# Residual rows and softmax sums turned by VectorE and DMA instead of TensorE in a two-layer hybrid trunk

## The chip, the core and the metric

The kernel runs on one core of a Trainium2 chip. The core has TensorE (PE, a 128x128 matmul array with its own weight loads, PEld), VectorE (DVE), ScalarE (ACT), GpSimd (POOL) and SyncE (SP), which here issues every DMA. SBUF and PSUM have 128 partitions; matmul results land in PSUM, in banks of 128 x 512 floats. The metric is the device time of one execution in microseconds (us), as the median of several runs.

## The reference

One sequence of 1024 tokens with 1024 features passes two layers. Layer 0 mixes by gated linear attention, layer 1 by sparse attention with an indexer that keeps the 256 best keys of every query; each is followed by a residual, a layer norm and a gated input of per-layer embeddings.

```python
for i in range(DEPTH):                       # DEPTH = 2
    y = gla_mixer(x, ...) if i == 0 else dsa_mixer(x, ...)
    x = layer_norm(ALPHA * x + y, ln_g[i], ln_b[i])      # ALPHA = 4 ** 0.25
    x = x + (p[i] @ ple_w[i]) * jax.nn.sigmoid(x @ ple_gate_w[i])
```

In the sparse attention, 16 heads of 128 share one key and one value head. For every head

```python
probs = jax.nn.softmax(logits, axis=-1)      # over the kept keys
o = probs @ v_sel
...
return (o * jax.nn.silu(z)) @ w_out          # over all 16 heads
```

All is float32 in and out.

## The kernel before, in words

**Numbers.** A float32 matmul is done as three matmuls of a faster 32-bit format: every operand is split into a high part (a ScalarE copy) and a low part (a VectorE subtraction), and hi*hi, hi*lo and lo*hi are added in PSUM. A *block* is one product of a 1024-row weight with 512 tokens: 8 x 3 = 24 matmuls of 512 columns (`fm_block`, L441).

**Order.** Tokens go in two halves of 512. Layer 0 runs half 0 and half 1, each as four heads (`v_phase`, `qk_phase`, `core_steps`, `out_phase`) and a `tail` (L905: layer norm applied, turned to features by rows, gate). After each tail come the indexer's and the shared key and value projections (`small_head` L1003, `small_kv` L1050). Then layer 1 runs half 0 and half 1, each as 17 slots and a tail. In a slot the head's attention steps lie between the projection blocks of other heads.

**The order is written by hand.** `Flow` (L48 on) keeps a clock `fl.now` that advances with the TensorE work issued so far, 512/2400 us for a matmul of 512 columns. Steps are put in a heap with a due time (`fl.at`, `after`, `chain`), and are issued between matmuls when `fl.now` has passed it and what they require is there (`fl.req`, `fl.ripe`); `fl.need` issues what is due later until a condition holds. Engines execute in the order of issue, so a step that waits holds what is behind it on its engine or queue. Weight tiles are loaded and split ahead of use by `Weights.pace`, at most two or three tiles ahead, through SP's queue. In layer 1 the weights come split already, from DRAM.

**The residual of layer 1.** The tail of layer 0 writes x2 (the input of layer 1) to DRAM by features, `x2s[k]` with k = 0..7, 128 features x 1024 tokens. Layer 1 adds its projections by tokens, to a tile `y` of 128 tokens x 4 x 1024. `residual` (L1489) loads two `x2s[k]` in each of the slots 0 to 3, turns each by four TensorE transposes into a PSUM bank (L1500) and copies them into `y` on ScalarE, times ALPHA (L1501). `accumulate` (L805) adds the projection on VectorE (L827), and `norm_steps` (L854) takes statistics (L869), powers on POOL (L863 to L866) and applies them in place, for two of the four token blocks on ScalarE (L877), for two on VectorE (L879). `xpose` in the tail (L916) turns the normalised `y` back by TensorE.

**The softmax sums.** A head's exponentials leave a sum per query in a 128x4 tile `sm`. `inverse` (L1602) takes reciprocals, `turn` transposes 128x4 to 4x128 on TensorE, ScalarE copies it out of PSUM (L1616), SP stores it to a DRAM `row` (L1617), and `to_all` (L1621) loads it back to all 128 partitions (L1625); the gate `z` is multiplied by it (L1647). `inverse` is due 3.0 before the end of the slot that computes the head's logits, `to_all` 3.5 (half 0) or 5.0 (half 1) into the next. A slot lasts 3.6 (half 0) or 8.6 (half 1) plus 5.12 for each block in it: two blocks in slots 0 to 3, three in slots 4 to 14.

**The pattern already used for squares.** In layer 0, `core_steps` turns an output of 128x512 as 32x32 squares on VectorE (L731), stores it by four DMAs, one for each 32 partitions (L750), and loads it back in one DMA (L756). The stores and the load put the squares in their places, and the reading instructions (L769 to L775) go by runs of 32.

**Start.** `start_half` (L1225) loads X by rows and the first two weight tiles, and the feeder splits X; with `feed_by(feeder, 0.0, 0.0)` (L1288) one row is issued at every step.

**Loads for layer 1's half 1.** `feed_x2` (L1481) loads `x2s[k]` one by one into a pair of buffers and splits them, beginning 21 us into the last projections of half 0.

## Time and profile before

| | us |
|---|---|
| median of 3 runs (1944.57 to 1944.95) | 1944.63 |
| the profiled execution | 1945.97 |
| its span, first to last instruction | 1944.2 |
| TensorE busy | 1924.8 |
| VectorE busy | 1481.8 |
| ScalarE busy | 1014.5 |
| POOL busy | 55.2 |

DMA moved 480.50 MB, 247 GB/s on average, all through SP's queue. The profile lists groups of instructions by line, engine and operation, with tile names: `out<-in`, shapes, count, busy time, mean length in ns, and the idle time of the engine ahead of them with what ended it. TensorE's instructions all stand on L58 (matmul) or L62 (transpose), so they are told apart by their tiles. Matmuls overlap: one of 512 columns lasts some 390 ns, and the next starts before it ends, so cost is read from start to start. In a timeline each row gives the start, the length, the engine, the line, the operation and, in brackets, the engine's idle time ahead of it with its releaser. SPq is SP's queue of DMA issues; a row's length there is the time to issue, not to move data.

### The profile page before, as it was taken

Reading aid. Unit: us, or ns where it says so; the run is one execution under the profiler, and the core shown is the slowest. Engines: PE = TensorE matmul, PEld = TensorE weight load, DVE = VectorE, ACT = ScalarE, POOL = GpSimd, SP = SyncE. Lnnn points to the kernel's source line nnn. Section 1 sums busy time; section 2 is a strip of 40 time slices with the busy share of each in tenths; the row PEclk is TensorE's granted clock in tenths of the full one; section 3 lists DMA queues with packets and bytes.
Section 4 is the critical chain, followed back from the end, with each engine's and each line's share of the span. In section 5 each row is a group of like instructions: output and inputs, shape, how many; then the busy total and the mean of one; then the engine's idle time right before and its main releaser. Section 6 shows DMA issues by size and latency. Waiting matters only on the chain.

```text
span 1944.2 us, 26708 instructions
## 1 busy us (share of the span) xinstructions
PE 1924.8 (99%) x8912; PEld 1596.4 (82%) x8912; DVE 1481.8 (76%) x3039; ACT 1014.5 (52%) x1930; POOL 55.2 (3%) x115
## 2 busy tenths in 40 slices
PE   9999999999999999999999999999999999999999
PEld 7888888888788888888888888888878888888877
DVE  5777666696778888888859987778797887777873
ACT  5564636445564646464635676766443554434432
POOL 0000000010000000000100000000000000000000
PEclk9999999999999999999999999999999999999999
DMA  4567776767668777677686588877867998888873
GB/s 155 201 222 229 221 226 214 227 210 268 227 196 266 226 212 233 220 226 218 207 304 222 194 308 292 276 271 259 317 221 236 365 323 300 299 297 300 294 260 144
DMA packets 195818, 480.50 MB, mean 247 GB/s; under 512 B 22496, under 2 KB 39008, under 8 KB 189536
## 3 DMA queue, kind: packets, MB, share of 16 engines
q1 hardware_dynamic: 195680, 478.79, 73.8%
q8 instruction: 70, 1.15, 0.2%
q14 instruction: 68, 0.56, 0.1%
HBM read 338.98 MB, written 139.72 MB: 246 GB/s over the span
## 4 chain that ended last, share of the span: by engine, by line
PE 88%; DVE 4%; ACT 4%; DMA 2%; issue 1%; SPq 0%; POOL 0%; ACTq 0%; DVEq 0%
PE pb L58 66%; PE o L58 8%; PE U L58 6%; PE S L58 6%; DMA wlo<-wls 1%; PE tr L58 1%; ACT x L926 1%; DVE wlo L191 0%; DVE bn L869 0%; DMA xst<-x2s 0%; DMA y<-in_x_T 0%; DVE y L827 0%; PE pb L62 0%; PE ix L58 0%; DMA row<-uf 0%
## 5 line engine op out<-in xcount | busy, mean ns | idle before, releaser
L58 PE MATMUL pb<-x,whi 128*128 128x512 f32 x2272 | 705.4, 391 | 1.1 <-DVE x L411 1.0
L58 PEld LDWEIGHTS pb<-x,whi 128*128 128x128 f32 x2272 | 418.2, 188 | 81.2 <-DVE x L411 2.2
L58 PE MATMUL pb<-x,wlo 128*128 128x512 f32 x1136 | 442.8, 390 | 0.0
L58 PE MATMUL pb<-whi,u 128*128 128x512 f32 x1024 | 339.9, 392 | 1.5 <-ACT u L419 0.8
L58 PEld LDWEIGHTS pb<-x,wlo 128*128 128x128 f32 x1136 | 213.2, 188 | 45.7 <-DVE wlo L191 0.4
L58 PEld LDWEIGHTS pb<-whi,u 128*128 128x128 f32 x1024 | 192.1, 188 | 41.4 <-ACT u L419 1.2
L58 PE MATMUL pb<-wlo,u 128*128 128x512 f32 x512 | 199.8, 390 | 0.5 <-DMA wlo<-wls 0.5
L191 DVE TENSOR_TENSOR wlo<-wst,whi 128x512 fp32r<-128x512 f32 x232 | 154.3, 684 | 37.5 <-ACT whi L189 37.4
L189 ACT ACTIVATE whi<-wst 128x512 fp32r<-128x512 f32 x232 | 136.5, 622 | 69.4 <-DMA wst<-in_g_k 23.5
L1553 ACT ACTIVATE sq<-P,mx 128x128 f32<-128x128 f32 (+7 forms) x128 | 98.9, 773 | 88.2 <-DVE mx L1546 67.5
L58 PE MATMUL S<-kT,q 128*128 128x512 f32 (+2 forms) x576 | 122.4, 342 | 0.0
L1599 ACT ACTIVATE ph<-PT 128x512 fp32r<-128x512 f32 (+2 forms) x160 | 86.6, 559 | 65.6 <-PE o L58 46.3
L58 PEld LDWEIGHTS S<-kT,q 128*128 128x128 f32 x576 | 100.8, 188 | 18.1 <-DVE mx L1546 0.7
L58 PEld LDWEIGHTS pb<-wlo,u 128*128 128x128 f32 x512 | 96.2, 188 | 19.3 <-DMA wlo<-wls 1.3
L1597 DVE TENSOR_TENSOR PT<-PT,ph 128x512 fp32r<-128x512 f32 (+2 forms) x160 | 93.3, 594 | 21.1 <-ACT ph L1599 20.7
L1180 ACT ACTIVATE tk<-sc,tki 128x768 f16<-128x768 f32 (+2 forms) x90 | 92.8, 1031 | 18.3 <-DVE tki L1189 16.1
L1559 DVE STREAM_TRANSPOSE sq<-sq 128x128 f32<-128x128 f32 (+7 forms) x128 | 97.6, 768 | 3.2 <-ACT sq L1553 3.0
L237 DVE TENSOR_TENSOR pst<-pst,phi 128x512 fp32r<-128x512 f32 x130 | 88.7, 683 | 7.5 <-ACT phi L233 7.4
L736 ACT ACTIVATE junk<-o 128x512 bf16<-128x512 f32 x32 | 19.1, 597 | 142.1 <-DVE ot L731 109.8
L58 PE MATMUL o<-ph,vT 128*128 128x512 f32 (+2 forms) x320 | 92.4, 370 | 0.2 <-ACT ph L1599 0.2
L58 PE MATMUL pb<-whi,x 128*128 128x512 f32 x256 | 85.2, 391 | 0.7 <-ACT whi L189 0.7
L58 PE MATMUL U<-whi,x 128*128 128x512 f32 x256 | 84.5, 389 | 0.0
(324 smaller groups left out, 3325.0 us busy)
## 6 DMA issues: line engine op xcount, KB each, us to landing
whi<-whs SPq DMA_DIRECT2D x128, 512.0 KB
wlo<-wls SPq DMA_DIRECT2D x128, 512.0 KB
sqd<-sq SPq DMA_DIRECT2D x192, 256.0 KB
PT<-sqd SPq DMA_DIRECT2D x48, 1024.0 KB
whs<-phi SPq DMA_DIRECT2D x130, 256.0 KB
wls<-pst SPq DMA_DIRECT2D x130, 256.0 KB
wst<-in_g_z SPq DMA_DIRECT2D x32, 512.0 KB
wst<-in_g_o SPq DMA_DIRECT2D x32, 512.0 KB
```

Source lines behind the costliest of these rows:

```text
L58: self.pe.matmul(out, lhsT, rhs, start=start, stop=stop)
L189: self.nc.scalar.activation(hi[:, c], st[:, c], AF.Copy, scale=1.0 if gain is None else gain)
L191: self.nc.vector.tensor_sub(lo[:, c], st[:, c], hi[:, c].bitcast(F32))
L237: self.nc.vector.tensor_sub(st, st.bitcast(F32), hi.bitcast(F32))
L736: act.activation(junk, ps, AF.Square, accum_out=u["ss"][:, c:c + 1])
L926: act.activation(X1[k], ps, AF.Identity, scale=g, bias=b)
L1180: act.activation(junk()[:, :n], scs[j], AF.Sign, bias=cand[:, j:j + 1].bitcast(F32), accum_out=cnt[:, j:j + 1])
L1553: act.activation(to, rows, AF.Exp, scale=-1.0, bias=mx, accum_out=sm[:, t:t + 1])
L1559: dve.transpose(x, x)
L1597: dve.tensor_sub(lo, lo.bitcast(F32), hi.bitcast(F32))
L1599: chain((0, lambda: act.activation(hi, lo.bitcast(F32), AF.Copy)), (0.8, second))
```

## The change

Seven things change together.

1. **Residual in squares.** VectorE turns each 128x512 of x2 as 32x32 squares (`in_squares`); POOL's queue stores it to DRAM by four DMAs (`by_rows`) and loads it back by one (`back`). For half 0 of layer 1 this is done up to the store in layer 0's half 1, two blocks at the start of each of its four heads (`rows_ahead`, in tiles that the head's state parts use later), and the loads come in slots -1 and 0 of layer 1. For half 1 all of it is done from slot -1 on, one block per 5.0, out of the tile from which X was split (`residual`). `y` is then in square order, read in runs of 32 through a function `y(t, a, n)`; it holds x2 without ALPHA, and EPS and the values' scale are divided accordingly.
2. **Softmax sums.** The reciprocals go into four columns of one of two kept 128x32 tiles, VectorE turns that as squares, and POOL stores 4x32 pieces by four DMAs; TensorE and ScalarE have no part. It is due 8.5 (half 0) or 12.0 (half 1) after the slot's start.
3. **Norm out of place.** Normalised rows go to tiles of X that are free by then, in two pieces of 512.
4. **`fm_two`.** The first two gate blocks of each tail, and the indexer's key block with the first query block, are computed in turns: the first 4 (5) of the 8 row blocks of both, then the rest of both.
5. **s3** of layer 0 waits until 2.2 instead of 1.6 after its input is issued.
6. **Start.** Rows 2 and 3 of X are loaded ahead of the second weight tile, and X is split one row per 1.3.
7. **X of layer 1's half 1** is loaded only when the norm of half 0 has been issued, into the whole `y` tile, one block per 2.3 with three loads ahead of the split.

```diff
+    def fm_two(keys, X, evacs, cut):
+        parts = [W.take(key) for key in keys]
+        banks = [pbank() for _ in keys]
+        for ks in (range(cut), range(cut, NK)):
+            for (hi, lo), ps, evac in zip(parts, banks, evacs):
+                for k in ks:
+                    xh, xl = X[k]
+                    at = slice(k * 128, k * 128 + 128)
+                    for i, (l, r) in enumerate(((hi, xh), (hi, xl), (lo, xh)), 3 * k):
+                        mm(ps, l[:, at], r, i == 0, i == 3 * NK - 1)
+                    if k < NK - 1:
+                        yield
+                if ks.stop == NK:
+                    evac(ps)
+                    yield
...
-                fl.ripe(st["At", c] + 1.6)
+                fl.ripe(st["At", c] + 2.2)
...
-            ys = y[:, t, ch * 512:ch * 512 + 512]
+            ys = y(t, ch * 512, 512)
...
-                dve.tensor_add(ys, ps, ys)
+                dve.tensor_add(ys, ps.rearrange("p (x i) -> p x i", i=32), ys)
...
-                if t in on_act:
-                    act.activation(y[:, t], y[:, t], AF.Identity, scale=rstd[:, t:t + 1], bias=mv[:, t, 1:2])
-                else:
-                    dve.tensor_scalar(y[:, t], y[:, t], mv[:, t, 0:1], rstd[:, t:t + 1],
-                                      op0=OP.subtract, op1=OP.mult)
+                for there, row in to(t):
+                    if t in on_act:
+                        act.activation(there, row, AF.Identity, scale=rstd[:, t:t + 1], bias=mv[:, t, 1:2])
+                    else:
+                        dve.tensor_scalar(there, row, mv[:, t, 0:1], rstd[:, t:t + 1],
+                                          op0=OP.subtract, op1=OP.mult)
...
+        yield from fm_two([("t", layer, b) for b in range(2)], X, [gate(b, False) for b in range(2)], 4)
...
+        yield from fm_two([("ki",), ("qi", 0)], X, [ev_ki, query(0)], 5)
...
+    def in_squares(sq, t):
+        dve.transpose(sq.rearrange("p (m b i) -> p b m i", m=4, b=4), t)
+    def by_rows(rd, sq):
+        for a in range(4):
+            pool.dma_start(rd[:, :, a].rearrange("m r x -> r m x"),
+                           sq[32 * a:32 * a + 32].rearrange("p (m x) -> p m x", m=4))
+    def back(st, y, k, rd):
+        pool.dma_start(y[:, k], rd.rearrange("m r a x -> (m r) (a x)"))
+        st["y"] = st.get("y", 0) + 1
+    def rows_ahead(k, i, start):
+        tiles = {}
+        def part(n):
+            tiles[n] = lp.tile([128, HT], F32, tag=f"S{n}{i}", name="xk")
+            return tiles[n]
+        def turn():
+            in_squares(part("l"), tiles["h"])
+            kept[k] = rows_tile(f"ys{k}")
+            after(1.0, lambda: by_rows(kept[k], tiles["l"]))
+        fl.at(start, lambda: pool.dma_start(part("h"), x2s[k, :, 0:HT]))
+        fl.at(start + 10.0, turn)
...
                 load(1, 1)
+                load(2, 2)
                 W.loads(W.ns + 2)
...
-            feed_by(feeder, 0.0, 0.0)
+            feed_by(feeder, 0.0, 1.3)
...
+            if half:
+                for i in range(2):
+                    rows_ahead(2 * h + i, i, fl.now + 6.0 + 4.0 * i)
...
+    def feed_x2(X, y_done, new_y):
+        for i in range(2):
+            nc.sync.dma_start(tabs[i], rope_s[i, 0:32, HT:2 * HT])
+        while not all(y_done):
+            yield
+        y = new_y()
+        for k in range(NK + 3):
+            if k < NK:
+                nc.sync.dma_start(y[:, k], x2s[k, :, HT:2 * HT])
+            if k > 2:
+                X.put(k - 3, y[:, k - 3])
+            yield
+    def residual(st, y, start, gap):
+        def turn(k):
+            sq = xp.tile([128, HT], F32, tag="xst", name="xst", bufs=2)
+            in_squares(sq, y[:, k])
+            after(1.0, lambda: away(k, sq))
+        def away(k, sq):
+            rd = rows_tile("rd", 4)
+            by_rows(rd, sq)
+            after(3.0, lambda: back(st, y, k, rd))
         for k in range(NK):
+            fl.at(start + gap * k, lambda k=k: turn(k))
...
-            dve.reciprocal(st["sm", h], st["sm", h])
-            after(1.5, turn)
-        def turn():
-            ps = spsum()
-            fl.transpose(ps[0:4, 0:128], st["sm", h], ident)
-            inv = tmp1()[0:4, 0:128]
+            sums = l1.tile([128, 32], F32, tag="bn", name="sums")
+            dve.reciprocal(inverses[h % 2][:, 0:4], st["sm", h])
+            dve.transpose(sums, inverses[h % 2])
             row = st["row", h] = dp.tile([4, 128], F32, tag="row", name="row", bufs=2)
             def out():
-                act.activation(inv, ps[0:4, 0:128], AF.Copy)
-                nc.sync.dma_start(row, inv)
+                for a in range(4):
+                    pool.dma_start(row[:, 32 * a:32 * a + 32], sums[32 * a:32 * a + 4])
                 st["r", h] = True
             after(0.5, out)
...
-                fl.at(start + dur - 3.0, scale[0])
+                fl.at(start + (12.0 if half else 8.5), scale[0])
...
+                if half:
+                    residual(st, yt, start + 0.5, 5.0)
+                else:
+                    for k in range(NK):
+                        fl.at(start + 14.0 + 3.0 * k, lambda k=k: back(st, yt, k, kept[k]))
```

More of the change, by code (lines that the diff above doesn't have):

```diff
@@ L940, in tail, with gate, ev @@
             yield
-        for b in range(NK):
-            def ev(ps, ts=slice(0, HT), b=b):
+        def gate(b, cut):
+            def ev(ps, ts=slice(0, HT)):
                 sg = tmp()[:, ts]
@@ L950, in ev @@
                       (1.5, lambda: final(b, x1, ts) if cut else final(b, x1)))
+            return ev
+        yield from fm_two([("t", layer, b) for b in range(2)], X, [gate(b, False) for b in range(2)], 4)
+        for b in range(2, NK):
             cut = split_last and b == NK - 1
-            yield from fm_block(("t", layer, b), X, ev, *([(slice(0, 256), slice(256, HT))] if cut else []))
+            yield from fm_block(("t", layer, b), X, gate(b, cut),
+                                *([(slice(0, 256), slice(256, HT))] if cut else []))
     def rope_tables():
@@ L1032, in weights, with query, ev_qi @@
             res["w"] = wt
-        yield from fm_block(("ki",), X, ev_ki)
-        for b in range(4):
-            def ev_qi(ps, b=b):
+        def query(b):
+            def ev_qi(ps):
                 qf = f32t()
@@ L1245, in feed @@
                 load(1, 1)
+                load(2, 2)
                 W.loads(W.ns + 2)
-                for k in range(2, NK, 2):
-                    load(k, 2)
+                load(4, 2)
+                load(6, 2)
                 nc.sync.dma_start(ba, g_ba)
@@ L1803, in trunk_kernel, with y, to_rows, rows @@
                             lambda k: xp.tile([128, HT], F32, tag="xst", name="xst", bufs=2))
[L1804 to L1807 removed]
+            if h == -1:
+                y5 = yt.rearrange("p k (a t i) -> p (k a) t i", a=4, t=4)
+                def y(t, a, n, y5=y5):
+                    return y5[:, a // 32:(a + n) // 32, t]
+                normed = {}
+                def to_rows(t, y=y, normed=normed):
+                    normed[t] = [xp.tile([128, HT], F32, tag="x", name="yn", bufs=16) for _ in range(2)]
+                    return [(r.rearrange("p (x i) -> p x i", i=32), y(t, 512 * i, 512)) for i, r in enumerate(normed[t])]
+                def rows(t, a, n, normed=normed):
+                    return normed[t][a // 512][:, a % 512:a % 512 + n]
+                if half:
[3 more added lines that the diff above has]
+                        fl.at(start + 14.0 + 3.0 * k, lambda k=k: back(st, yt, k, kept[k]))
             fl.run(*(unit(u) for u in units))
[L1809 removed]
+        norm, y_done = norm_steps(y, l1, EPS / ALPHA ** 2, to_rows, (0, 1))
         if half == 0:
             X = XT()
[L1812 removed]
+            def next_y():
+                nonlocal yt
+                yt = new_y()
+                return yt
+            feed_by(feed_x2(X, y_done, next_y), fl.now + 21.0, 2.3)
         for u in last_outs:
@@ L1821, in trunk_kernel @@
         gx = gate_tiles(tp)
-        tail_gen = tail(1, Pt, y, y_done, lambda b, t, ts=slice(0, HT), at=half * HT: nc.sync.dma_start(
+        tail_gen = tail(1, Pt, rows, y_done, lambda b, t, ts=slice(0, HT), at=half * HT: nc.sync.dma_start(
                             out[b * 128:(b + 1) * 128, at + ts.start:at + ts.stop], t),
```

66 lines of the change are left out of this document (19 added, 47 removed).

## The prediction

> **What bounds the kernel now.** First the page's totals, then its chain of work that ended last.
>
> ```profile
> span 1944.2 us, 26708 instructions
> PE 1924.8 (99%) x8912; PEld 1596.4 (82%) x8912; DVE 1481.8 (76%) x3039; ACT 1014.5 (52%) x1930; POOL 55.2 (3%) x115
> ...
> PE 88%; DVE 4%; ACT 4%; DMA 2%; issue 1%; SPq 0%; POOL 0%; ACTq 0%; DVEq 0%
> ```
>
> TensorE is busy 99% of the span and carries 88% of the chain. So a TensorE instruction that disappears is time off the end, and work that moves to VectorE (76%), POOL or DMA is free as long as no TensorE instruction starts later for it. The granted clock is 1.000 throughout. I need TensorE's own beat, from the chain in order of time:
>
> ```profile
> 25.17 2.72 PE pb L58 x12
> ```
>
> Twelve matmuls of 512 columns in 2.72 us: 0.227 us each. Below, a gap is what start-to-start times hold beyond this.
>
> **The change part by part.**
>
> *Residual.* The TensorE groups by shape, and one group of four residual transposes in the timeline (start, length, what, how many):
>
> ```profile
> L62 PE MATMUL pb<-ident,xst 128*128 128x128 f32 x64 | 9.6, 273 | 1.0 <-DMA xst<-x2s 1.0
> ...
> 1554.73 0.62 PE L58 MATMUL o<-ph,vT 128*128 128x512 f32 x2
> 1555.18 0.39 PE L58 MATMUL o<-PT,vT 128*128 128x512 f32 x1
> 1555.42 0.60 PE L62 MATMUL pb<-ident,xst 128*128 128x128 f32 x4
> 1555.77 0.71 PE L58 MATMUL o<-ph,vT 128*128 128x512 f32 x2
> 1556.32 0.40 PE L58 MATMUL o<-PT,vT 128*128 128x512 f32 x1
> 1556.55 0.62 PE L58 MATMUL o<-ph,vT 128*128 128x512 f32 x2
> ```
>
> From 1554.73 to 1556.55 are 1.82 us with six matmuls (1.36), so four transposes cost 0.46. Sixteen such groups (8 blocks, two halves) go: 16 x 0.46 = **7.4 us**; between 16 x 0.35 = 5.6 (first transpose to the next matmul's start) and the group's busy 9.6. With them goes the 1.0 us that TensorE waited for a residual load: **1.0**.
>
> In their place come 16 VectorE transposes in squares, eight in layer 0's half 1 and eight in layer 1's half 1, and DMAs, all on POOL: per block four stores and one load, and in layer 0 a first load, 8 + 32 + 8 and 32 + 8 in all. SP loses 16 loads. The same pattern is in the kernel already:
>
> ```profile
> L731 DVE STREAM_TRANSPOSE ot<-o 128x512 f32<-128x512 f32 x29 | 20.8, 716 | 22.4 <-PE o L58 22.2
> ```
>
> 16 x 0.72 = 11.5 us on VectorE, spread over some 400 us and some 40 us; ScalarE loses 16 copies from PSUM. I cost this at nothing. Its cover is VectorE's free time; in the busier place, 42 us at the head of layer 1's half 1, VectorE was busy 29.26:
>
> ```profile
> GB/s 155 201 222 229 221 226 214 227 210 268 227 196 266 226 212 233 220 226 218 207 304 222 194 308 292 276 271 259 317 221 236 365 323 300 299 297 300 294 260 144
> ...
> 1470.00:1512.00 42.00, 42.00 (x195) 35.17 (x195) 29.26 (x63) 16.36 (x30) 2.03 (x1) 1.00 0.78 269
> ```
>
> Eight transposes make 35 of 42 (columns: stretch, length, PE, PEld, DVE, ACT, POOL busy, clock, DMA share, GB/s; the first line is the page's GB/s by slice). Without the cover it is at most 8 x 0.72 = 5.7. Two trips of 256 KB for each of eight blocks are 4 MB in 42 us, 100 GB/s more; with 269 that is about what the busiest slice moved, 365: tight, not over it.
>
> *Softmax sums.* One of the 32 single transposes:
>
> ```profile
> 1377.48 0.34 PE L58 MATMUL o<-PT,vT 128*128 128x384 f32 x1
> 1377.65 0.27 PE L62 MATMUL S<-ident,sm 128*4 128x128 f32 x1
> 1377.68 0.71 PE L58 MATMUL pb<-x,whi 128*128 128x512 f32 x2
> 1378.22 0.40 PE L58 MATMUL pb<-x,wlo 128*128 128x512 f32 x1
> 1378.46 0.39 PE L58 MATMUL o<-PT,vT 128*128 128x128 f32 x2
> ```
>
> 1377.48 to 1378.46 are 0.98: one matmul of 384 columns (three quarters of a beat, 0.17), three of 512 (0.68), so 0.13 is the transpose. 32 x 0.13 = **4.2**, between 1.0 (0.03 to the next start) and a whole beat each, 7.3. Added are 32 VectorE transposes of 128x32, each below the 0.72 of a 128x512, and 128 POOL stores for 32 on SP.
>
> *When the sums leave.* The recurring hand-over, on SP's queue:
>
> ```profile
> L1617 SPq DMA_DIRECT2D row<-uf x32: 256/277/1572, 1086.5 to 1854.1; - x32
> ...
> 1382.20 0.28 SPq L1617 DMA_DIRECT2D row<-uf  x1
> 1386.75 0.32 SPq L1625 DMA_DIRECT2D inv<-row  x1
> ...
> 1394.48 0.39 PE L58 MATMUL pb<-whi,u 128*128 128x512 f32 x1
> 1395.10 0.50 PE L58 MATMUL pb<-wlo,u 128*128 128x512 f32 x1 [0.23 <-DMA wlo<-wls]
> ```
>
> (The first line is that store's issue on SP, ns least/median/most.) SP stands 4.5 us at the broadcast until the row has landed; the weight loads queue behind it; TensorE then loses 1395.10 - 1394.48 - 0.227 = 0.39. The change reads the sums at 8.5 (half 1: 12.0) after the slot's start and broadcasts, as now, at 3.5 (5.0) in the next. In half 0's shortest slots (two blocks of 5.12 and 3.6, 13.84 of the planner's time, whose beat is 0.213 for 0.227) that leaves 13.84 + 3.5 - 9.0 = 8.3, or 8.8 us. Four stores and a landing of 4.5 fit if a store holds POOL under 1.08 us. No row shows a DMA issued by POOL; the nearest are SP's issues, 0.28 at the median and 1.57 at most. I take 0.7, between the two: just in time. Worth the 0.39 in each half: **0.6** (0 to 0.8).
>
> The Trainium skill ("DMA: Bandwidth & Descriptors", Anatomy of one DMA — SWDGE (gpsimd) path) gives a POOL-issued DMA a fixed cost of about 2.0 us, mostly completion; by it the row would land sooner than the 4.5 here and the sum stays. No run so far shows it.
>
> *Two blocks in turns (fm_two).* The gate blocks of the tail want X[4..7] half a block later. In layer 1's half 0:
>
> ```profile
> 1422.33 0.40 PE L58 MATMUL pb<-gx,whi 128*128 128x512 f32 x1
> 1422.96 0.50 PE L58 MATMUL pb<-gx,whi 128*128 128x512 f32 x1 [0.24 <-DVE gx L411]
> ...
> 1423.53 1.04 PE L58 MATMUL pb<-gx,whi 128*128 128x512 f32 x2
> 1424.40 0.39 PE L58 MATMUL pb<-gx,wlo 128*128 128x512 f32 x1
> 1424.67 0.49 PE L58 MATMUL pb<-gx,whi 128*128 128x512 f32 x1
> 1425.73 0.50 PE L58 MATMUL pb<-gx,whi 128*128 128x512 f32 x1 [0.57 <-DVE gx L411]
> ```
>
> Gaps 0.40 + 0.42 + 0.83 = **1.65**. The second half of the contraction moves back by 12 matmuls, 2.7 us, more than the three gaps together, so all of it goes and no later split is missed. For the other tails and the indexer's head I count nothing.
>
> *Start.* Rows 2 and 3 of X come ahead of the second weight tile, and X is split one row per 1.3 instead of at once:
>
> ```profile
> 12.44 0.39 PE L58 MATMUL pb<-whi,x 128*128 128x512 f32 x1
> 13.07 0.50 PE L58 MATMUL pb<-wlo,x 128*128 128x512 f32 x1 [0.24 <-DVE wlo L191]
> 13.41 0.63 PE L58 MATMUL pb<-whi,x 128*128 128x512 f32 x2
> 14.88 0.50 PE L58 MATMUL pb<-wlo,x 128*128 128x512 f32 x1 [0.84 <-DVE wlo L191]
> ```
>
> Gaps 0.40 and 1.02: the weight's low part stands behind X's splits on VectorE. The spacing frees it, but its own load is now one later: **0.8** (0 to 1.4).
>
> *Rest.* That s3 waits 2.2 for A's parts moves its matmuls behind others of the same length: nothing. The normalised rows go out of place in two pieces each: two of 512 for one of 1024. Square-wise order costs VectorE nothing where it is read already in runs of 32:
>
> ```profile
> L775 DVE TENSOR_TENSOR uf<-uf,z 128x512 f32<-128x512 f32 x29 | 19.8, 683 | 4.2 <-DMA uf<-od 4.2
> L869 DVE BATCH_NORM_STATS2 bn<-y 128x6 f32<-128x512 f32 x32 | 22.2, 694 | 1.1
> L827 DVE TENSOR_TENSOR y<-pb,y 128x512 f32<-128x512 f32 x80 | 54.2, 678 | 22.2 <-PE pb L58 21.5
> ```
>
> 683 ns against 678. The loads of the second half's X in layer 1 begin only after the norm and go twice as densely; the first use is a whole tail later (eight gate blocks of 24 beats, 43.6 us). Nothing.
>
> **Sum.** 7.4 + 1.0 + 4.2 + 0.6 + 1.65 + 0.8 = 15.65. The planner, which counts time by matmuls, packs everything anew; for waits that move I take off 0.65, an estimate of the size of one or two of the gaps above: **-15.0**. The profiled execution took 1945.97 (span 1944.2 and 1.77 around it), 1.34 over the median of the three runs, 1944.63. So 1931.0 for a profiled run, **1929.6** for the median.
>
> **Rivals.**
>
> *Sums late (gain partly lost).* A row speaks against POOL's DMAs beside VectorE:
>
> ```profile
> 426.54 0.76 DVE L879 TENSOR_SCALAR y<-y,mv,rstd 128x1024 f32<-128x1024 f32 x1
> ...
> 430.57 0.95 POOL L462 MEMSET wah<- 128x1024 f32 x1
> 430.65 1.41 DVE L879 TENSOR_SCALAR y<-y,mv,rstd 128x1024 f32<-128x1024 f32 x1 [0.44 <-POOL rstd L864]
> ```
>
> The same VectorE instruction takes 1.41 instead of 0.76 while POOL writes. If it goes the other way too and each store waits out one such instruction, four take 4 x (0.7 + 0.76) = 5.8, the row lands after 10.3 and is 1.5 late in the short slots; at SP's slowest issue, 1.57, it is 2.0 late. Also for: POOL runs in order, and a load back stands there until its stores have landed, with the sums behind it. Against: 4.5 us of SP's wait cost TensorE only 0.39. At 0.4 in each of 16 heads of one half, 6.4 lost: 1936. The Trainium skill ("SBUF — State Buffer", SBUF: two separate sides) says that VectorE and POOL share a port pair as an exclusive lock, and that a POOL-issued DMA starves for descriptors while VectorE runs a two-port instruction; the row agrees as far as the lock goes.
>
> *POOL's queue becomes the bound (slower).* At the head of layer 1's half 1 each block holds POOL for four stores, the rest of a landing and a load, one block every 5.0 of the planner's time, 5.3 us. With 0.7 a DMA and a landing of 4.5, of which the planned gap covers 3.2, that is 2.8 + 1.3 + 0.7 = 4.8; at 1.57 it is 9.2. Beyond 5.3 the backlog after eight blocks is 8 x the excess, and the first heads' sums stand behind it. Their room there is 18.84 + 5.0 - 12.5 = 11.3, 12 us; past that SP stops, and two staged blocks of weights last another 11. At 13 us a block 62 - 23 = 39 are lost: 1969. It decides for slower from 10 us a block: 38 - 23 = 15, the whole gain. Against: the rows are half of that.
>
> *TensorE's time comes back as waits (no change).* The removed 11.6 us lie in slots where VectorE, ScalarE and DMA share the chain 10%; if those ends stay put, 1944. Against: TensorE showed no gap in 42 of 42 us above.
>
> *Last projection bound by VectorE.* There an add and a statistic, 0.68 + 0.69, stand against six matmuls, 1.36. Were runs of 32 10% slower there, 16 pairs would lose 2.2: 1931.8.
>
> **How the numbers follow.** Forecast 64%; sums late 16%; last projection 6%; no change 6%; slower 8%. Faster by over 0.2% (3.9 us, about what a measurement can tell) is 86%, same 6%, slower 8%. All terms high (9.6 + 7.3 + 1 + 0.8 + 1.65 + 1.4) give -21.75, 1923; all low (5.6 + 1.0 + 1 + 1.65) give -9, 1935, and the late sums reach 1936: 1923 to 1937, which leaves out the no-change and slower cases.
>
> **What would show it.** TensorE has 96 instructions fewer and some 11 us less busy; no gap at 1422 to 1426 or 13 to 15 in their counterparts; SP's broadcast directly behind its neighbours. Wrong would be: TensorE idle on weight loads early in layer 1's half 1, POOL stores above 1 us, the broadcast held over 4 us, adds of y above 0.72.

## The result and the profile after

The changed kernel takes 1958.42 us (median of 4 runs, 1954.43 to 1960.58) against 1944.60 (4 runs) of the kernel before beside it: 1.0069 times as long, 95% interval 1.0052 to 1.0087. It is slower by 13.8 us, where 15.0 less were forecast. In what follows a "difference" is the median of a kernel less the median of the kernel before in the same comparison. The intervals reach 1.7 us to each side where a kernel ran ten times or more, and up to 3.4 where it ran four times; so a step between two differences is told apart from nothing only from about 2.5 us on, from about 4.5 between two kernels of four runs, and what is smaller leans on the traces. A few single executions, among them the profiled one of e12_lighter, ran at 2 to 3.5 times the length whatever the kernel; the ratios leave them out, and the medians shift by 0.12 us at most with them.

The page of the profiled execution after (1960.58 us), totals and chain:

```profile
span 1958.8 us, 26890 instructions
PE 1924.9 (98%) x8816; PEld 1597.0 (82%) x8816; DVE 1497.2 (76%) x3091; ACT 1000.5 (51%) x1886; POOL 168.0 (9%) x333
...
PEclk9999999999999999999999999999998999999999
...
PE 84%; DVE 6%; DMA 4%; ACT 3%; issue 2%; POOL 1%; SPq 1%; DVEq 0%; POOLq 0%; ACTq 0%
PE pb L58 64%; PE o L58 7%; PE U L58 6%; PE S L58 5%; DMA rd<-xst 2%; DMA PT<-sqd 1%; PE tr L58 1%; DVE sq L1611 1%; DVE PT L1649 1%; POOL rd L1260 1%; DMA inv<-row 0%; DMA wst<-in_g_v 0%; DVE wlo L191 0%; PE xt L62 0%; PE ix L58 0%
```

96 TensorE instructions are gone (8912 to 8816), as the change says. But TensorE's share of the chain fell from 88% to 84%, and what came in is VectorE, DMA and POOL: by line the residual's stores (rd<-xst 2%, POOL rd 1%), the load of PT and the turns of sq. The one slice with an 8 under PEclk is 1469 to 1518, the head of layer 1's half 1. The stretch around it in both kernels (columns as in the prediction's window):

```profile
1470.00:1620.00 150.00, 150.00 (x722) 125.65 (x722) 122.74 (x258) 71.37 (x136) 2.03 (x1) 1.00 0.90 315
```

That was before. After:

```profile
1470.00:1620.00 150.00, 136.28 (x599) 110.67 (x598) 118.75 (x250) 59.03 (x109) 37.69 (x65) 0.95 0.87 297
```

TensorE was never idle there before; after, it is idle for 13.7 of 150 us and issues 599 instructions instead of 722 (38 of the missing ones are transposes, the rest is work that slips behind the stretch). All engines but POOL do less; so does the DMA. Something is being waited for. VectorE's timeline in that stretch (start, length, engine, line, what, and in brackets the idle time before it and what ended it):

```profile
1499.55 0.71 DVE L1256 STREAM_TRANSPOSE xst<-y 128x512 f32<-128x512 f32 x1 [4.00 <-DMA rd<-xst]
1500.19 0.65 DVE L411 TENSOR_TENSOR q<-qf,q 128x512 fp32r<-128x512 f32 x1
1500.76 0.68 DVE L1526 SCALAR_TENSOR_TENSOR z<-z,pb 128x512 f32<-128x512 f32 x1
1508.37 0.71 DVE L1256 STREAM_TRANSPOSE xst<-y 128x512 f32<-128x512 f32 x1 [6.93 <-DMA rd<-xst]
1509.01 0.52 DVE L1598 CUSTOM_DVE_ANT_0 P<-S,bias 128x384 f32<-128x384 f32 x1
```

and TensorE's:

```profile
1497.78 0.51 PE L58 MATMUL S<-kT,q 128*128 128x384 f32 x2
1500.89 0.96 PE L58 MATMUL S<-kT,q 128*128 128x384 f32 x4 [2.60 <-DVE q L411]
1501.65 1.05 PE L58 MATMUL pb<-x,whi 128*128 128x512 f32 x2
1502.51 0.63 PE L58 MATMUL pb<-x,wlo 128*128 128x512 f32 x1
...
1505.29 0.40 PE L58 MATMUL pb<-x,wlo 128*128 128x512 f32 x1
1509.59 2.61 PE L58 MATMUL S<-kT,q 128*128 128x512 f32 x6 [3.91 <-DVE mx L1598]
```

The rows show VectorE taking its instructions in the order in which they were issued. The turn of a residual block into one of the two xst tiles stands still until POOL's stores of the block two before have landed, 4.00 and 6.93 us. Right behind it stand the split of q and the P of the attention, and TensorE waits 2.60 and 3.91 us for just these. The waits of the stretch 1470 to 1620 (what waited, for what, us in total, times, longest), first those of POOL, VectorE and ScalarE, then SP's queue:

```profile
POOL y L1264 <- DMA rd<-xst: 28.9, 6, 7.0
...
DVE xst L1256 <- DMA rd<-xst: 16.4, 6, 6.9
ACT sq L1605 <- DMA sqd<-sq: 13.9, 3, 7.4
...
POOL row L1664 <- DMA y<-rd: 4.6, 2, 3.1
```

```profile
SPq L1672 <- DMA row<-sums: 12.6, 4, 9.2
```

POOL holds each load back until its stores have landed, the rows of sums stand behind that, and SP stands up to 9.2 us at the broadcast. SP stands there in other kernels too, so the total alone is no price. In the same stretch of the kernel before, and of e8_both_pe, the fastest kernel but for its two lighter variants (below):

```profile
SPq L1625 <- DMA row<-uf: 10.5, 6, 3.0
...
SPq L1675 <- DMA row<-uf: 27.9, 6, 5.2
```

What is new after the change is the length of a single wait. Three candidates, then, all from the residual's way by POOL: the two tiles, POOL's queue, and the traffic. Where the rest went, by two marks of TensorE's timeline in the profiled executions (single ones; seven kernels of this study with the same code in the middle stage lie between 349.4 and 354.4 there):

| stage | before | changed kernel | e4_res_pe | e8_both_pe | e10_no_two |
|---|---|---|---|---|---|
| start to layer 1's first S<-kT,q | 1068.48 | 1066.64 | 1066.35 | 1065.37 | 1066.27 |
| from there to the first pb<-gx (tail of half 0) | 351.78 | 354.35 | 351.40 | 348.88 | 347.98 |
| from there to the end of the span | 523.94 | 537.81 | 526.85 | 524.25 | 526.55 |

Of the 14.6 us between the spans, -1.8 lie ahead of layer 1's attention, +2.6 in its half 0 (no more than the scatter of that stage) and +13.9 behind it. The gaps of before at 1406 and 1422 to 1426 are gone.

### The profile page after: what moved, and what is told of

It reads as the page before. It is cut to its first block, busy times and chain, and to the rows that moved or that the text cites. A ratio compares the mean times of both kernels' runs of the same rounds, so it can differ in the third digit from the quotient of the medians.

```text
span 1958.8 us, 26890 instructions
## 1 busy us (share of the span) xinstructions
PE 1924.9 (98%) x8816; PEld 1597.0 (82%) x8816; DVE 1497.2 (76%) x3091; ACT 1000.5 (51%) x1886; POOL 168.0 (9%) x333
## 4 chain that ended last, share of the span: by engine, by line
PE 84%; DVE 6%; DMA 4%; ACT 3%; issue 2%; POOL 1%; SPq 1%; DVEq 0%; POOLq 0%; ACTq 0%
PE pb L58 64%; PE o L58 7%; PE U L58 6%; PE S L58 5%; DMA rd<-xst 2%; DMA PT<-sqd 1%; PE tr L58 1%; DVE sq L1611 1%; DVE PT L1649 1%; POOL rd L1260 1%; DMA inv<-row 0%; DMA wst<-in_g_v 0%; DVE wlo L191 0%; PE xt L62 0%; PE ix L58 0%
## 5 line engine op out<-in xcount | busy, mean ns | idle before, releaser
L58 PE MATMUL S<-kT,q 128*128 128x512 f32 (+2 forms) x576 | 127.5, 352 | 9.8 <-DVE q L411 5.2
L1664 POOL DMA_DIRECT2D row<-sums x128 | 63.5, 503 | 590.3 <-DVE sums L1659 535.5
```

The source lines that it names most:

```text
L58: self.pe.matmul(out, lhsT, rhs, start=start, stop=stop)
L1664: pool.dma_start(row[:, 32 * a:32 * a + 32], sums[32 * a:32 * a + 4])
```

## The experiments

All times with the kernel before beside them:

| run | us | difference | ratio, 95% interval |
|---|---|---|---|
| changed kernel | 1958.42 | +13.8 | 1.0069 (1.0052 to 1.0087) |
| e1_eight | 1956.90 | +11.8 | 1.0061 (1.0045 to 1.0077) |
| e2_gap10 | 1949.74 | +4.6 | 1.0026 (1.0015 to 1.0037) |
| e3_sums_pe | 1954.68 | +9.6 | 1.0054 (1.0038 to 1.0070) |
| e4_res_pe | 1946.03 | +0.9 | 1.0008 (0.9999 to 1.0018) |
| e5_turn_only | 1943.80 | -1.1 | 0.9992 (0.9983 to 1.0002) |
| e6_dma_only | 1953.35 | +8.5 | 1.0042 (1.0027 to 1.0057) |
| e7_late_read | 1943.21 | -1.7 | 0.9991 (0.9981 to 1.0001) |
| e8_both_pe | 1941.02 | -3.9 | 0.9982 (0.9973 to 0.9991) |
| e9_rows_sp | 1950.94 | +5.9 | 1.0033 (1.0020 to 1.0047) |
| e10_no_two | 1943.35 | -1.7 | 0.9992 (0.9983 to 1.0001) |
| e11_direct | 1944.82 | -0.2 | 0.9997 (0.9989 to 1.0006) |
| e12_lighter | 1940.92 | -4.4 | 0.9978 (0.9969 to 0.9987) |
| e13_late_sp | 1944.52 | -1.2 | 0.9997 (0.9988 to 1.0006) |
| e14_also_dve | 1943.41 | -2.3 | 0.9988 (0.9979 to 0.9997) |
| e15_lighter_again | 1941.25 | -4.5 | 0.9977 (0.9968 to 0.9986) |

**e1_eight: eight tiles instead of two.**

```
+        sqs = [ap.tile([128, HT], F32, tag="u", name="xsq", bufs=10) for _ in range(NK)]
         def turn(k):
-            sq = xp.tile([128, HT], F32, tag="xst", name="xst", bufs=2)
+            sq = sqs[k]
```

> Eight tiles of their own for the turned squares of layer 1's half 1 (taken from the u tiles, which are free there); the order, the stores and the loads on POOL and the 5.0 between blocks stay. Theory V (VectorE, which works in order, stands at the third and each later turn until POOL's stores of the block two before have landed, and the attention's work stands behind it): VectorE waits for nothing named xst or xsq, and the gaps of TensorE between 1470 and 1550 (15 us) and some 2 us behind them go: 1943 us, 1940 to 1946. Rival Q (POOL's queue itself is the bound, through the softmax sums that stand in it): POOL's work is the same, so nothing changes: 1957 to 1960. Rival C (the DMAs beside TensorE lower its granted clock): the same DMAs, so 1957 to 1960 with a granted clock of 0.8 still in that slice.

Measured: 1956.90, +11.8, 2.0 less than the changed kernel, which is within the measurement. Theory V, the reading that the timeline suggested, falls as the whole cause: VectorE waits for no xsq any more, and TensorE is idle all the same, now for other things. Its waits in 1470 to 1620:

```profile
ACT sq L1607 <- DMA sqd<-sq: 21.3, 3, 11.1
...
ACT ph L1653 <- DMA PT<-sqd: 14.9, 5, 6.6
```

```profile
SPq L1674 <- DMA row<-sums: 21.7, 4, 10.2
```

ScalarE waits longer than after for the stores of sq and for PT, and SP's time at the broadcast rose from 12.6 to 21.7 us. Taking the loudest wait away handed the time to the next one.

**e2_gap10: a block every 10.0 instead of 5.0.**

```
-                    residual(st, yt, start + 0.5, 5.0)
+                    residual(st, yt, start + 0.5, 10.0)
```

> Two tiles as in the kernel after, but a block every 10.0 of the planner's time instead of 5.0. Theory V: the stores of block k have landed before block k+2 is turned (20 planned against 2 x 8 to 9 measured), so VectorE doesn't wait and the same 15 to 17 us come back: 1941 to 1946. Rival Q: POOL's queue has room too, so the same: 1941 to 1946; the two are told apart by the other run. Rival C: the same bytes in twice the time, about half of the loss stays: 1950.

Measured: 1949.74, +4.6, the number that rival C gave (1950), and short of V and Q. C's mechanism is not seen: with the same bytes the granted clock from 1470 to 1620 is 1.00 here, at 321 GB/s, so the DMAs alone do not lower it. Half the rate gives back 9.2 of what the residual costs, not all of it. It gives room to POOL's queue and to the traffic alike and doesn't tell the two apart.

**e3_sums_pe: the sums as before.**

```
-            sums = l1.tile([128, 32], F32, tag="bn", name="sums")
-            dve.reciprocal(inverses[h % 2][:, 0:4], st["sm", h])
-            dve.transpose(sums, inverses[h % 2])
+            dve.reciprocal(st["sm", h], st["sm", h])
+            after(1.5, turn)
...
-                    pool.dma_start(row[:, 32 * a:32 * a + 32], sums[32 * a:32 * a + 4])
+                act.activation(inv, ps[0:4, 0:128], AF.Copy)
+                nc.sync.dma_start(row, inv)
...
-                fl.at(start + (12.0 if half else 8.5), scale[0])
+                fl.at(start + dur - 3.0, scale[0])
```

> The softmax sums as in the kernel before: reciprocal, transpose by TensorE, copy by ScalarE, one store on SP, read dur - 3.0 after the slot's start; the residual stays as in the kernel after. Theory S (the sums' new place and the four POOL stores cause the gaps of layer 1's half 0, 8 us at 1116 to 1183 and 1.4 at 1381): these go and the 32 transposes come back, 4.2: 1953. Rival P (the half 0 gaps are the planner's order, moved by the TensorE time that the residual no longer takes, whatever the sums do): they stay and the transposes are added: 1962. Half 1's head keeps its 15 us in both.

Measured: 1954.68, +9.6: 4.2 faster with 32 transposes more on TensorE. That is theory S by its number, though between two kernels of four runs 4.2 is not quite clear of the measurement (e4 to e8 below, 4.8, is). By its place only in part: half 0's stage is 348.0, where the seven kernels with the changed sums have 349.4 to 354.4, the gaps at 1160 and 1381 went, but of 2.28 us at 1116 1.37 stayed, and at 1173 a gap of 1.75 is there.

**e4_res_pe: half 1's residual turned by TensorE.**

```
         def turn(k):
-            in_squares(sq, y[:, k])
-            after(1.0, lambda: away(k, sq))
+            ps = pbank()
+            for t in range(4):
+                fl.transpose(ps[:, t * 128:t * 128 + 128], y[:, k, t * 128:t * 128 + 128], ident)
+            act.activation(y[:, k].rearrange("p (a t i) -> p t a i", a=4, t=4),
+                           ps.rearrange("p (t a i) -> p t a i", t=4, a=4), AF.Copy)
+            st["y"] = st.get("y", 0) + 1
```

> Only layer 1's half 1: the residual turned by TensorE again (four transposes a block from the tile that is there already, one copy by ScalarE in squares' order), no POOL DMA and no VectorE turn there; half 0 keeps the rows turned in layer 0. Theory V: the head of half 1 loses nothing but the transposes, 8 x 0.46 = 3.7: 1958 - 17 + 3.7 = 1945. Rival Q says the same, 1945. Rival that half 1's head loses its time to something else than the residual (the sums on POOL): 1958 to 1962.

Measured: 1946.03, as expected. Half 1's residual by VectorE, POOL and DMA costs 13.8 - 0.9 = 12.9 us more than 32 TensorE transposes, which are 3.7 by the prediction's price; its whole price is so 16.6.

**e5_turn_only and e6_dma_only: the two halves of that way, each alone.**

```
 e5      def turn(k):
             in_squares(sq, y[:, k])
-            after(1.0, lambda: away(k, sq))
+            st["y"] = st.get("y", 0) + 1
```

```
 e6      def turn(k):
-            in_squares(sq, y[:, k])
-            after(1.0, lambda: away(k, sq))
+            after(1.0, lambda: away(k, y[:, k]))
```

> As e1_eight (eight tiles), but in layer 1's half 1 only VectorE's eight turns are left; the stores, the loads back and their waits are left out, so the rows of y are not the residual by token. Eight tiles did not bring the time back, so two theories are open for the head of half 1. Theory D (the residual's DMAs: beside them the stores of sq and the loads of PT land later, and the row of the sums stands behind them in POOL's queue): the gaps of TensorE between 1470 and 1620, 16 us in e1_eight, go: 1942 us, 1939 to 1945. Theory T (the 8 x 0.72 us of VectorE stand ahead of the attention's parts where VectorE is already dense): they stay: 1953 to 1958.

> The other half: the stores and loads back on POOL as in e1_eight, taken from y itself, and no turn by VectorE in layer 1's half 1 (the rows of y are not turned by it). Theory D: the gaps stay, 1953 to 1958. Theory T: 1942. If both runs come to some 1949, each carries a half.

e5 uses e1's eight tiles and leaves out the stores and loads back; e6 leaves out the turn and its tiles. Measured: 1943.80 and 1953.35. Theory D: the DMAs carry it, the turns little. In e6 no VectorE turn is there, and ScalarE waits twice as long for the stores of sq as before the change (13.2 in 4 waits, below):

```profile
ACT sq L1603 <- DMA sqd<-sq: 28.1, 4, 11.5
...
ACT ph L1649 <- DMA PT<-sqd: 12.7, 6, 4.6
```

The same waits in the kernel before:

```profile
ACT sq L1553 <- DMA sqd<-sq: 13.2, 4, 4.0
...
ACT ph L1599 <- DMA PT<-sqd: 3.3, 2, 2.5
```

and its DMA throughput from 1480 to 1560, in 40 slices of 2 us:

```profile
GB/s 231 2 0 295 234 95 209 286 263 241 225 344 420 417 430 416 406 396 408 367 252 321 359 385 416 383 295 399 368 293 264 218 345 396 423 409 407 370 323 302
```

The attention moves its squares out and PT in by bursts: for 14 us on end (1504 to 1518) it already moved 396 to 430 GB/s. In e6 one such slice reaches 444. What the residual moves in such a burst puts off what the burst carries: from 1470 to 1620 ScalarE waits 9.2 to 16.4 us for PT in five kernels with the residual's DMAs (e1, e2, e6, e9, e11), 6.6 and 6.7 in the two where VectorE stands at the two tiles (the changed kernel, e3), and 3.1 to 6.1 in the nine without them (before, e4, e5, e7, e8, e10, e13 to e15). TensorE waits for PT 5.2 to 11.6 us, 6.0 and 4.9, and 3.4 at most. The Trainium skill ("DMA: Bandwidth & Descriptors", Issuing engines are not separate DMA queues) says that DMAs started by any engine run on the same 16 DMA engines and interleave; the waits of e6 agree. The same page (Where 436 GB/s comes from) gives a ceiling of 435.2 GB/s for the ports to SBUF; that slice of e6 lies 2% above it.

**e9_rows_sp: half 1's rows of sums stored by SP (on e1's eight tiles).**

```
-                    pool.dma_start(row[...], sums[...])
+                    (nc.sync if half else pool).dma_start(row[...], sums[...])
```

> As e1_eight (eight tiles, the residual's DMAs on POOL), with half 1's rows of sums stored by SP instead of POOL, so that they no longer stand behind the residual in POOL's queue. e5 and e6 put 13 us on the DMAs. Theory Q2 (POOL's queue: the sums behind the residual's stores and loads come late, SP waits at the broadcast, and PT and the weights behind it): most of the 13 go: 1944 to 1947. Theory C2 (the traffic: 4 MB in the same 40 us make the stores of sq and the loads of PT land later, whoever issues the sums): 1954 to 1958.

Measured: 1950.94, +5.9, between the two theories: each carries a part. Against e1_eight 5.9 us come back, and SP's wait at the broadcast goes from 21.7, 10.2 at the longest, to

```profile
SPq L1674 <- DMA row<-sums: 0.6, 2, 0.4
```

ScalarE's wait for PT stays, 16.4 us in 6 waits. What is left against e5 (-1.1) is 7.0. That is all that the stores and loads do beside holding up the rows of sums; we put it down to the traffic, by ScalarE's and TensorE's waits for PT, not by a run that varies the traffic alone.

**e7_late_read and e8_both_pe.** On e4_res_pe, the sums read at dur - 3.0 again (e7), and the sums wholly as before (e8, the edits of e3 and e4 together).

> As e4_res_pe (half 1's residual by TensorE), with the sums still turned by VectorE and stored by POOL, but read dur - 3.0 after the slot's start as in the kernel before. In e4_res_pe the gaps of TensorE in layer 1's half 0 are some 7 us above those of before. Theory W (the earlier reading puts reciprocal and turn ahead of other work of VectorE at the wrong place): they go, 1940. Rival (the path by POOL, four stores and their landing): they stay or grow, 1946 to 1950. Rival (the planner's order, moved by any change): anywhere between, with other gaps in other places.

> Half 1's residual by TensorE (3.7 us) and the sums by TensorE as in the kernel before (4.2 us): left of the change are the rows turned in layer 0 for half 0, the two blocks in turns and the start. If the two edits add as they did apart (1946.0 from e4_res_pe, 3.7 less from e3_sums_pe): 1942.3. By the terms of the prediction alone, before less 3.7, 1.0, 1.65: 1938.7.

Measured: 1943.21 and 1941.02. Reading early costs 2.6 us (e4 to e7), at the edge of the measurement. Three of TensorE's waits of half 0 shrink in e7's trace: at 1160 from 1.28 to 0.73, at 1178 from 1.33 to 1.02 (both for PT) and at 1380 from 1.50 to 0.53 (for z), 1.8 together; the one for q at 1119 stays, 2.09 and 2.11. That is theory W in part. Yet e8, with 32 transposes more on TensorE than e7, is another 2.2 faster, within the measurement. e4 to e8, 4.8, is clear of it. e8_both_pe beats both kernels: 0.9982 of before.

**e10_no_two: e8 without the two blocks in turns.**

```
-        yield from fm_two([("t", layer, b) for b in range(2)], X, [gate(b, False) for b in range(2)], 4)
-        for b in range(2, NK):
+        for b in range(NK):
...
-        yield from fm_two([("ki",), ("qi", 0)], X, [ev_ki, query(0)], 5)
-        for b in range(1, 4):
+        yield from fm_block(("ki",), X, ev_ki)
+        for b in range(4):
```

> As e8_both_pe without the two blocks in turns, in both tails and at the indexer's head. By the prediction's step: 1.65 more; by the gaps that the trace of before has and after has not (0.40, 0.42 and 0.83 at 1422 to 1426, 0.88 at 1406): 2.5 more than e8_both_pe, 1943.5; if what goes there comes back elsewhere: the same 1941.

Measured: 1943.35, 2.2 more than e8 by the differences, between the 1.65 and the 2.5, and by itself within the measurement. Gaps on gx are back at 1417 and 1418 (0.49 and 0.57).

**e11_direct: no trip through DRAM.** On e8, half 1's blocks turned by VectorE into eight tiles, one every 10.0, and then

```
+            for a in range(4):
+                for m in range(4):
+                    pool.dma_start(y[32 * m:32 * m + 32, k, 128 * a:128 * a + 128],
+                                   sq[32 * a:32 * a + 32, 128 * m:128 * m + 128])
```

> As e8_both_pe, but half 1's residual turned by VectorE in eight tiles, a block every 10.0, and moved from the squares straight into y by 16 small stores on POOL, with no trip through DRAM and no load back: half the bytes, and nothing on VectorE or POOL waits for a landing; the sums by TensorE and SP. If the traffic and its waits were the price, it keeps the 3.7 us of transposes and loses some 1 to 2 to VectorE: 1938.5 to 1940. If small stores disturb as much: 1945 to 1950. Issuing takes POOL some 16 x 0.55 = 8.8 of every 10.6 us.

Measured: 1944.82, 3.7 worse than e8 by the differences, at the lower end of "small stores disturb as much". Half the bytes and no wait for a landing on POOL or VectorE, and ScalarE waits 21.7 us for the stores of sq and 14.0 for PT, where e8 has 8.7 and 4.4. Whether it is the number of small pieces or their bytes was not separated.

**e13_late_sp and e14_also_dve: why the sums cost.** e13 is e7 with the rows stored by SP; e14 is e8 with one VectorE transpose of 128x32 a head more, whose result nobody reads.

> As e7_late_read (sums turned by VectorE, read at dur - 3.0, half 1's residual by TensorE), with the four stores of each row on SP instead of POOL. If POOL's way makes the sums late (0.5 us and more for each store, then a longer landing): most of the 6 us come back, 1938 to 1940. If the loss is VectorE's, or SP's queue suffers from 96 more stores: 1943 or more.

> As e8_both_pe, with one more VectorE transpose of 128x32 for each head at the place where the kernel after has it; its result is not used. It is 0.21 us long and there are 32. If a turn costs what it lasts because VectorE is dense there: up to 6.7 us in all, and some 2 if only in half 0's first slots: 1943 to 1947. If it is hidden: 1941.

Measured: 1944.52 and 1943.41. SP instead of POOL brings nothing (-1.2 against -1.7), so in these kernels the sums' way by POOL is not what costs. The turn alone costs 1.5 (e8 to e14; 2.2 against e15 of the same comparison), which is within the measurement; half 0's first gap, at 1116, hardly grows by it (TensorE waits 1.28 for q there, 1.19 in e8). And e7 is e14 without its 32 TensorE transposes and ScalarE copies, with the rows by POOL: -1.7 against -2.3. Taking the 4.2 us of transposes away gained nothing that can be measured: in e7's trace TensorE waits 2.11 for q in that place, and 0.73 for PT at 1160 where e14 shows no wait.

**e12_lighter and e15_lighter_again: less for VectorE early in half 0.**

```
-            bg.gap = 1.4 if h == 15 else 1.75 if h > 3 and h % 4 < 2 else 1.5
+            bg.gap = 1.4 if h == 15 else 1.9 if h < 2 else 1.75 if h > 3 and h % 4 < 2 else 1.42
```

> As e8_both_pe with the background search of layer 1's half 0 (VectorE) a step every 1.9 instead of 1.5 in the first three slots, and every 1.42 instead of 1.5 in later ones. In before, VectorE is busy 33.4 of 35 us at 1085 to 1120; e8_both_pe has gaps of 1.36 at 1116 (q) and 1.79 at 1173 (PT) there. Theory L (half 0's early gaps are VectorE's work there, which the transposes of the residual had only covered: TensorE time taken away there comes back as waits): lighter there, the gaps go: 1938 to 1939. Rival (the gaps are a wrong order, not a lack of VectorE time): they stay, 1941. Rival (the steps put off make VectorE late further on): 1942 to 1944.

> e12_lighter again, for its trace: 1941. Theory L: the gaps at 1116 and 1173 are smaller than 1.36 and 1.79 by more than half, and what they gave is lost later in half 0. Rival: they are as large as in e8_both_pe.

Measured: 1940.92 and 1941.25, e8 within the measurement. In the trace the gap at 1173 (1.79 in e8) is gone and that at 1116 is as large as it was, 1.42; gaps of 1.35 and 1.01 stand at 1591 and 1602 instead of 0.82. Half 0's stage is 1.2 us shorter than in e8, the one behind it 2.1 longer, with the same code there. So theory L holds for one gap of two, and nothing is gained; what took the time later is not settled.

## Why the prediction was wrong, point by point

The prediction's terms against what the runs put on them (steps from one kernel to the next, from before to changed, so that they add up to the 13.8):

| term | predicted | measured | by |
|---|---|---|---|
| half 1's residual: transposes gone | -3.7 | -3.7 (the price taken over) | trace of before |
| half 1's residual: what comes in their place | 0 | +16.6 | e4 to changed kernel |
| softmax sums, with "leave earlier" | -4.2 - 0.6 | +4.8 | e8 to e4 |
| half 0's residual, its load wait, the start, and the parts put at nothing | -3.7 - 1.0 - 0.8 | -1.7 | before to e10 |
| two blocks in turns | -1.65 | -2.2 | e10 to e8 |
| planner | +0.65 | in the other rows | |

**The step that failed** is "I cost this at nothing. Its cover is VectorE's free time" (29.26 of 42 us were busy), with its ceiling "Without the cover it is at most 8 x 0.72 = 5.7". It priced the turn and not what the turn waits for and what its DMAs meet. The 16.6 us split along the runs: 2.0 for the two tiles (changed kernel to e1), 5.9 for the sums behind the residual in POOL's queue (e1 to e9), 7.0 for the rest of the DMAs, put down to the traffic (e9 to e5), and 1.7 for the turns themselves (e5 to e4 without its 3.7). Of these 5.9 and 7.0 are clear of the measurement. The last stage of the profiled executions alone (537.81, 539.15, 535.26, 524.79, 526.85 less 3.7) gives -1.3, 3.9, 10.5 and 1.6: queue and traffic stand, the two tiles and the turns are not told apart from nothing. The turns are the only part that the step had looked at, and there the runs don't contradict it. Some of these shares are a lower clock and not waits (last section). The order in which causes are removed decides their shares: VectorE's wait for the two tiles is 16.4 us in the trace and some 2 or less in the sum, since queue and traffic stand behind it.

**The traffic** was weighed: "with 269 that is about what the busiest slice moved, 365: tight, not over it". That took a mean over 42 us and a slice of 48.6 us. In 2 us slices the kernel before already had a burst of 396 to 430 from 1504 to 1518, and the residual's DMAs, issued from 1477 to 1540, fell into it.

**The rival of POOL's queue** named the right queue, and was dismissed by its size: 4.8 us a block by its rows, slower only from 10 us on. POOL's timeline after:

```profile
1492.87 0.57 POOL L1264 DMA_DIRECT2D y<-rd  x1 [3.61 <-DMA rd<-xst]
1493.43 2.19 POOL L1260 DMA_DIRECT2D rd<-xst  x4
1500.20 0.57 POOL L1264 DMA_DIRECT2D y<-rd  x1 [4.58 <-DMA rd<-xst]
1500.77 2.19 POOL L1260 DMA_DIRECT2D rd<-xst  x4
1502.96 1.53 POOL L1664 DMA_DIRECT2D row<-sums  x3
1505.98 0.50 POOL L1664 DMA_DIRECT2D row<-sums  x1 [1.49 <-DMA y<-rd]
1509.08 0.58 POOL L1264 DMA_DIRECT2D y<-rd  x1 [2.59 <-DMA rd<-xst]
```

From load to load are 7.3 and 8.9 us. A store takes 0.55 of POOL, below the 0.7 assumed, and SP's slowest 1.57 was no guide; the issue was priced well. The landing was not: 5.8 at the median for rd<-xst, where 4.5 had been taken, and POOL stands in it, 28.9 us in all. And the rival let a delay count only once 23 us of room were used up: by that rule the 7.3 to 8.9 a block, 2.0 to 3.6 beyond the 5.3, would have cost 0 to 6 over eight blocks. There was no such room: SP stood up to 9.2 us at the broadcast, where before it was 3.0 at most, with weights and PT behind it. The rival "Sums late" had named this wait ("a load back stands there until its stores have landed, with the sums behind it"). Its price, 6.4, is near the 5.9 of e1 to e9 by chance: it spread 0.4 over each of 16 heads, while TensorE has no idle time from 1620 to 1770 in either of these two kernels.

**The sums.** "32 x 0.13 = 4.2" may be the right price of a transpose, but it is the wrong worth of it: e14 to e7 gained nothing. The turn on VectorE (0.21 us each, 6.8 us in all) cost 1.5 to 2.2 by the medians, within the measurement, where it was counted as free, and the earlier reading, which was to bring 0.6, cost 2.6. The rival "TensorE's time comes back as waits" held here. The early slots of half 0 suggest why. The kernel before there:

```profile
1085.00:1120.00 35.00, 35.00 (x168) 29.28 (x167) 33.37 (x78) 18.15 (x39) 0.00 (x0) 1.00 0.68 229
```

VectorE was busy 33.37 of 35 us; the page's 76% hides it. From 1114 to 1165 stood half 0's eight groups of residual transposes, and every head has its sums. Without them TensorE comes earlier and VectorE doesn't. In e8_both_pe, which has only the residual's gone:

```profile
1115.85 0.40 PE L58 MATMUL S<-kT,q 128*128 128x256 f32 x2
1117.44 0.74 PE L58 MATMUL S<-kT,q 128*128 128x256 f32 x4 [1.19 <-DVE q L411]
```

VectorE runs without a pause up to that split of q, which ends at 1117.38, and TensorE stands 1.36 us; the other new gap, at 1173, is 1.79. What e15 adds speaks only half for it: with less work for VectorE there the second gap goes and the first stays. How the earlier reading makes its 2.6 us was not followed beyond the three waits named under e7.

**Half 0's residual.** The rows turned ahead in layer 0 cost nothing that shows there: up to layer 1's attention the kernels of the table of stages are 1.8 to 3.1 us shorter, 0.69 of it by the wait for A's low part at 894, which is gone with the later s3 and which the prediction had at nothing. Half 0's stage in e10 is 3.8 shorter than before, of the 4.7 forecast (3.7 + 1.0); the two new gaps stand against gaps of before that went. But the last stage of e10, with the same TensorE work as before, is 2.6 longer. That is the planner's term, which had been set at 0.65 from the size of one gap, or one of the parts put at nothing (the norm out of place, the later loads of X); no run separates them. Single profiled executions differ by a us or two in such a stage (e8 and e15: 524.25 and 526.31), so these parts are rough; the -1.7 of e10 is their sum by the medians.

**Two blocks in turns** agrees: 1.65 against 2.2, and in the traces the stretch from 1400 to 1440 holds 1.7 us more of gaps in e10 than in e8.

**The start** brought nothing. The splits are freer, but the second weight's last low part comes when it came before (14.88 in the prediction's row):

```profile
13.65 0.49 PE L58 MATMUL pb<-wlo,x 128*128 128x512 f32 x1 [0.83 <-DVE wlo L191]
13.99 0.63 PE L58 MATMUL pb<-whi,x 128*128 128x512 f32 x2
14.86 0.51 PE L58 MATMUL pb<-wlo,x 128*128 128x512 f32 x1 [0.24 <-DVE wlo L191]
```

The load that is one later is the bound: ScalarE stands 3.45 us for it (7.67 to 11.12) ahead of its next copy of X, and VectorE 3.04 for that copy. This is the lower end of the range that was given for the term.

**The last projection** was right: its adds in squares' order take as long as before.

```profile
L844 DVE TENSOR_TENSOR y<-pb,y 128x512 f32<-128x512 f32 x80 | 54.0, 676 | 23.4 <-PE pb L58 23.1
...
L886 DVE BATCH_NORM_STATS2 bn<-y 128x6 f32<-128x512 f32 x32 | 22.2, 694 | 1.1
```

**What was to show it.** Of the signs named, 96 instructions fewer came, TensorE's busy time did not fall (1924.9 for 1924.8; matmuls that start behind a wait or run at the lower clock, below, last longer), and of the signs of being wrong one came true: the broadcast held over 4 us, up to 9.2. As a sign it was weak, since the prediction's own row from before shows 4.5. TensorE's idle time early in half 1 ended on VectorE, not on weight loads. Of the two rules of the Trainium skill that the prediction weighed, the short fixed cost of a POOL-issued DMA ("DMA: Bandwidth & Descriptors", Anatomy of one DMA, about 2.0 us) was not met: the rows of 0.5 KB took 3.7 us at the median. That such DMAs starve behind VectorE ("SBUF — State Buffer", SBUF: two separate sides) doesn't show in the issue: 0.50 and 0.56 us on average, 0.65 at most, with VectorE busy at 76%. Whether it lengthens a landing no run separates.

## What to carry to other kernels

Before moving work off the bound engine, follow the moved work to its end: what its first instruction waits for (here the landing of a store, since the tiles were two), what stands behind that instruction on an engine that works in order, and which queue its DMAs share with something that the bound engine needs soon. Judge free engine and DMA time in slices as short as the step itself: 76% and 269 GB/s on average were 95% and 430 in the stretches that counted. And when one wait is removed and the time stays, the next wait had been there all along; only taking out the whole way (e4_res_pe) and then its parts told what each was worth.

## What the hardware showed beyond that

After gaps of together some 2 us TensorE ran at half speed for a few us, in some executions. In the changed kernel at 1176 to 1186 two gaps, 0.54 and 1.61 us, lie within 3 us, and then:

```profile
1181.53 1.05 PE L58 MATMUL pb<-whi,u 128*128 128x512 f32 x2
1182.39 0.63 PE L58 MATMUL pb<-wlo,u 128*128 128x512 f32 x1
1182.81 1.05 PE L58 MATMUL pb<-whi,u 128*128 128x512 f32 x2
1183.67 0.51 PE L58 MATMUL pb<-wlo,u 128*128 128x512 f32 x1
```

1181.53 to 1182.81 are three matmuls in 1.28 us, 0.43 each where the beat is 0.227, with nothing waited for; from 1184 on the clock is 1.00 again. The granted clock of that stretch is the column before the last two:

```profile
1176.00:1186.00 10.00, 8.29 (x29) 6.09 (x29) 8.85 (x22) 5.64 (x11) 2.00 (x4) 0.83 0.77 214
```

It is 0.95 over 1470 to 1620 and 0.995 over the whole run, where before it is 1.000. That bounds what this adds to the waits: 0.005 x 1958.8 = 9.8 us. The four runs of the changed kernel line up with it: 1954.43 us at 0.997, 1957.46 at 0.996, 1959.38 and 1960.58 at 0.995. So part of the 13.8, at most 6 to 10 us, is not waiting but slow matmuls behind waits; the split above (profiled executions: e1 at 0.997, e9, e5 and e4 at 0.999) doesn't take it out. It also differs from run to run: e1_eight has the same gaps at 1115 and 1175, 2.25 and 1.62 us, with no slow matmuls behind them, and the changed kernel's four runs spread over 6.2 us. The Trainium skill ("TensorE: Matmul & The Clock Gate", What's actually happening) has a gate that halves the clock after an idle window of some 3.4 us and opens after as long a busy one, in a window that runs free of the program. The half speed and the spread agree; here shorter gaps were enough.
